# An encoder block: where the forms of the conv rows are made, when raw weights are queued, and how chains of weights are spaced

## The chip, the cores and the metric

The kernel runs on one core of one Trainium2 chip. The metric is device microseconds of one execution; the median of several runs is compared. The engines are TensorE (PE, with its weight loads PEld), VectorE (DVE), ScalarE (ACT), GpSimd (POOL) and SyncE (SP). In this kernel every DMA is issued by SP. Each engine takes its instructions in the order in which the program wrote them, and an instruction that waits for another engine or for a DMA holds up what is behind it on its own engine.

## The reference

One layer on 1024 tokens of width 1024, in float32. What the document needs of it:

```python
u = RMSNorm(x)
q, k, v, cb, cc, ch, ga, gb = split(u @ w_in)
y_a = neighbourhood_attention(q, k, v, rpb) @ w_attn_branch     # 8 heads x 64
y_b = (cb * conv3(cc * ch, conv_w)) @ w_conv_branch             # depthwise, width 3, 512 channels
merged = sigmoid(ga) * y_a + sigmoid(gb) * y_b
x = x + merged @ w_o
x = x + relu(RMSNorm(x) @ w_mlp_in) ** 2 @ w_mlp_out
```

## The kernel before

Every float32 operand is scaled by a power of two and held as two float16 halves, high and low. A product takes three passes of float16 matmuls: high by high, and each high by the other's low. Many products are also done in seven block products in place of eight. For those, both operands are first brought into seven *forms*: four quarters and some of their sums and differences, each split into high and low. The function `seven` runs the seven products of one gate chunk, and its posts add the results up.

The program runs through these stages: norm and the V, Q and K projections (to about 150 us), attention with the conv projections filled in between its steps (to about 315 us), then the stage that the change is about (315 to 572 us: the gates, the two branches and their merging), then W_o, then the MLP. The stage behind attention goes round by round. `gate_units(n)` (line 1444) makes the sigmoid gates of 128 channels out of the chunk S(n), by seven units of twelve matmuls of 128x512. `ab(j)` (line 1538) does the two branches for 256 channels: four A units of twelve matmuls, and seven B units of six matmuls, whose operands are the seven forms of the conv rows. For j from 0 to 2 the order is gate 2j+1, `ab(j)`, gate 2j+2; `ab(3)` follows gate 6, and gate 7 ends the stage.

A unit of work is issued by `unit` (line 235). It writes the matmuls, counts their columns in `work[0]`, writes the posts of the unit before (`settle`), and then calls some `step`s and `tick`s. A step advances every generator in the list `fg`. A tick advances the first generator in the list `bg`; if it answers WAIT, the next one is tried. So a generator's yields decide behind which unit its next instructions stand. `apart(mark, n, of)` answers WAIT until the counter `of` has grown by n; with `of = work` that is a number of columns, and 6144 columns are one unit of twelve matmuls. When the program reaches a point that needs a chunk of weights, `built(chunk)` sets `forced[0]` and ticks until that chunk is split. While forced, `apart` and `aged` don't wait.

The weights come in chunks. Per chunk: `load_upto` (line 263) queues raw loads on SP into five raw buffers of 128x1024 float32. Then `prep_s` (1351, gate chunks S), `prep_b` (1376, chunks B of the conv branch) or `Chunk.prep` with `largest` (361, chunks A of the attention branch) takes the squares or maxima, sums them over the partitions by a matmul with ones (`all_sum`, line 229 in the profile), makes a power of two, makes sums of quarters on POOL (lines 1317 and 1403) and splits into high (ACT, line 1335) and low (DVE, line 1331). `prep_s` and `prep_b` wait until all earlier chunks are done. `aged` (1181) holds a chunk until the columns since its load was queued reach three units.

The conv rows, 512 channels by 1024 tokens, are kept as two halves (a = 0, 1) of four quarters each. Each half becomes seven forms. `hi` (926) copies to float16 on ACT, `lo` (929) subtracts on DVE or POOL, and `put` (932) writes the form to a DRAM buffer `bf`. `land` (1484) reads a form of both halves back from `bf` to one of four slots of `bT`, in the order in which the B units need them: the first four after all forms are put, and each further one after the B unit that used the slot before. Before the change `conv_early` makes three forms of half 0 within attention, staged in `kD`; `conv_late`, advanced one segment a step behind attention, makes the other eleven, with staging tiles in `zb` and `mL` (`M[1]`). Four places in `zb` serve for half 0 first and then for half 1, so that the second use waits for the put of the first. `turn_s(0, 2)` (1301) puts eight DMA transposes on SP's queue between the first and second gate unit.

Of the kernel before, what the change touches and what calls it, by code (L numbers as in the profile page):

```python
# [15 lines left out]
OP = mybir.AluOpType  # L16
# [85 lines left out]
def encoder_block(ctx: ExitStack, tc: tile.TileContext, x, weights, cols, gqk, rel, masks, out):  # L102
# [132 lines left out]
    def unit(mms, post=None, steps=0, ticks=0):  # L235

        for ps, l, r, a, b in mms:
            T.matmul(ps, l, r, start=a, stop=b)  # L238
        units[0] += 1
        work[0] += len(mms) * mms[0][0].shape[-1]  # L240
        settle()
# [17 lines left out]
    def load_into(t, ch, p):  # L259
        m = ch.widths[p][0] * ch.widths[p][1]  # L260
        SP.dma_start(t, bass.AP(tensor=weights.tensor, offset=weights.offset + ch.offs[p], ap=[[m, 128], [1, m]]))
# [631 lines left out]
    SLOT = BTF.rearrange("p (n a w t) -> p n a w t", n=4, a=2, w=2)  # L893
    KS = KD[:, 0:2].rearrange("p a w t -> p (a w t)").rearrange("p (n w t) -> p n w t", n=4, w=2)
    BF = dram.tile([128, 7, 2, 2, 512], F16, name="bf")
    cm, crow, form_tail, formed, rowed = keep(2), at(rowsB, 2, 2), [], [False] * 2, [False]

# [3 lines left out]
    def conv_split(j):  # L901
# [31 lines left out]

    def conv_early():
        (e0, e1), (o0, o1) = quarters(0)
        conv_scaled(0)
        yield
        yield
        for i, v in enumerate((o1, e0, o0)):
            hi(KS[:, i], v)  # L940
            yield
            lo(KS[:, i], v, G)
            yield
        G.tensor_tensor(o1, e1, o1, op=OP.subtract)
        yield
        G.tensor_tensor(e1, e0, e1, op=OP.subtract)
        for i, f in enumerate((3, 0, 1)):
            put(KS[:, i], f, 0)
            yield

    def conv_late():

        zs = zb.rearrange("p n t -> p (n t)").bitcast(F16).rearrange("p (n w t) -> p n w t", n=4, w=2)
        ms = M[1][:, 2:6].rearrange("p n (w t) -> p n w t", w=2)
        (e0, e1), (o0, o1) = quarters(0)
        V.tensor_tensor(e0, o1, e0, op=OP.subtract)
        V.tensor_tensor(o0, o0, e0, op=OP.add)
        conv_scaled(1)
        hi(zs[:, 0], o1), hi(zs[:, 1], e1)
        yield  # L960
        (p0, p1), (q0, q1) = quarters(1)
        V.tensor_tensor(zs[:, 0, 1], o1, zs[:, 0, 0], op=OP.subtract)
        V.tensor_tensor(zs[:, 1, 1], e1, zs[:, 1, 0], op=OP.subtract)
        hi(zs[:, 2], e0), hi(zs[:, 3], o0)
        yield
        lo(zs[:, 2], e0, V), lo(zs[:, 3], o0, V)
        yield
        put(zs[:, 0], 2, 0), put(zs[:, 1], 5, 0)
        hi(ms[:, 0], q1), hi(ms[:, 1], p0), hi(ms[:, 2], q0)
        yield  # L970
        put(zs[:, 2], 4, 0), put(zs[:, 3], 6, 0)
        formed[0] = True
        lo(ms[:, 0], q1, V), lo(ms[:, 1], p0, G), lo(ms[:, 2], q0, G)
        V.tensor_tensor(q1, p1, q1, op=OP.subtract)
        yield
        yield
        V.tensor_tensor(p1, p0, p1, op=OP.subtract)
        V.tensor_tensor(p0, q1, p0, op=OP.subtract)
        hi(ms[:, 3], q1)
        yield  # L980
        put(ms[:, 0], 3, 1), put(ms[:, 1], 0, 1), put(ms[:, 2], 1, 1)
        V.tensor_tensor(q0, q0, p0, op=OP.add)
        hi(zs[:, 0], p1), hi(zs[:, 1], p0)
        yield
        lo(ms[:, 3], q1, V), lo(zs[:, 0], p1, V)
        hi(zs[:, 2], q0)
        yield
        lo(zs[:, 1], p0, V), lo(zs[:, 2], q0, V)
        yield
        put(ms[:, 3], 2, 1), put(zs[:, 0], 5, 1)  # L990
        yield
        put(zs[:, 1], 4, 1), put(zs[:, 2], 6, 1)
        formed[1] = True
# [49 lines left out]
    st = {}  # L1043
# [137 lines left out]
    def aged(ch, i):  # L1181
        return forced[0] or i >= len(ch.when) or work[0] >= ch.when[i] + 3 * 6144

# [44 lines left out]
    def deal(k):  # L1228
        room = 216.0 * share(k) + 520.0
        if conv_tail and not advance(conv_tail[0]):  # L1230
            conv_tail.pop(0)
        if form_tail and not advance(form_tail[0]):
            form_tail.pop(0)
# [51 lines left out]
    V, A = nc.vector, nc.scalar  # L1285
    assert not form_tail and rowed[0]
    solo[0] = False
# [63 lines left out]
    def prep_s(n):  # L1351
# [6 lines left out]
        else:  # L1358
# [10 lines left out]
        yield  # L1369
        ch.P = wsp.tile([128, 7, 2, 512], F16, name="w16_s", tag="ws")  # L1370
# [5 lines left out]
    def prep_b(j):  # L1376
# [10 lines left out]
        yield  # L1387
# [16 lines left out]
        yield  # L1404
        yield
        yield from parts([x for a in range(2) for x in ((place(3, 5, a), w[:, 0, :, a]), (place(5, 7, a), w[:, 1, :, a]))],
# [174 lines left out]
    fg.append(first_forms())  # L1581
    bg.append(prep_s(1))
    bg.append(prep_b(0))
    for j in range(1, 4):
# [6 lines left out]
    sgs[0] = gate_units(0)  # L1591
    gates[0] = 1
    built(cA[0])
# [63 lines left out]
    flush()  # L1657
    side[0] = False

# [616 lines left out]
```

## Time and profile before

| | us |
|---|---|
| median of 3 runs | 1240.71 (1240.1 to 1242.06) |
| the profiled execution, its time | 1241.13 |
| the profiled execution, its span | 1239.4 |
| TensorE busy in it | 1199.1 (97%) |
| DVE, ACT, POOL busy in it | 963.5, 778.1, 486.0 |

The profile is one execution. Its page has the busy time of each engine, a picture of the span in 40 slices, the chain of work that ended last, and the costliest groups of instructions; further views list a stretch of time row by row. A timeline row has its start and its duration in us, the engine, the line in the kernel, the operation, what it writes and reads, its shape, how many instructions it stands for, and in brackets how long the engine was idle before it and what ended that. SPq is the queue of SP: a transfer stands there from the first issue to the last one of its group. PEclk is the clock that TensorE was granted, as a share of full speed. The forms of a matmul with ones (line 229) are small, but TensorE waits for their input like for any other.

### The profile page before, as it was taken

How to read it: one execution, taken by the hardware profiler on the slowest of the kernel's cores; microseconds unless marked ns; L12 is line 12 of the kernel's file. 1: busy time of each engine (PE TensorE's matmuls, PEld its weight loads, DVE VectorE, ACT ScalarE, POOL GpSimd, SP SyncE). 2: the span in 40 equal slices, each digit the busy share in tenths (PEclk: the TensorE clock that was granted, in tenths of full speed). 3: DMA queues.
4: the chain of work that ended last, by engine and by line, in shares of the span. 5: the costliest groups of instructions: out<-in, count | busy, mean ns of one | idle time of the engine just before them, and what ended most of it. 6: DMA issues, size and time to landing. Idle time of an engine off the chain costs nothing.

```text
span 1239.4 us, 17137 instructions
## 1 busy us (share of the span) xinstructions
PE 1199.1 (97%) x6248; PEld 576.3 (46%) x6248; DVE 963.5 (78%) x1790; ACT 778.1 (63%) x1241; POOL 486.0 (39%) x317
## 2 busy tenths in 40 slices
PE   8999999999887789999999999999999999999998
PEld 7444445445433334444448544444444444444444
DVE  7987788888767677688788755554547999999998
ACT  7775678777565546244677877877857663545430
POOL 5610021231333243220002666556557564474472
PEclk9999999999988889999999999999999999999999
DMA  7755646777664142326169454543575843436212
GB/s 261 204 147 111 117 105 122 156 168 129 158 214 159 52 169 68 120 103 235 37 119 205 143 184 158 187 147 134 187 259 191 292 170 131 180 106 251 81 55 103
DMA packets 168373, 189.62 MB, mean 153 GB/s; under 512 B 123616, under 2 KB 124128, under 8 KB 164192
## 3 DMA queue, kind: packets, MB, share of 16 engines
q1 hardware_dynamic: 168288, 188.52, 51.0%
q8 instruction: 49, 0.80, 0.3%
q14 instruction: 36, 0.29, 0.1%
HBM read 117.19 MB, written 41.42 MB: 128 GB/s over the span
## 4 chain that ended last, share of the span: by engine, by line
PE 79%; DVE 10%; ACT 5%; POOL 2%; DMA 1%; issue 1%; SPq 1%; ACTq 0%; POOLq 0%; DVEq 0%
PE ps_d L238 24%; PE ps_s L238 20%; PE ps_o L238 18%; PE ps_d L1156 9%; PE ps_d L675 2%; PE ps_d L724 2%; PE ps_s L724 2%; PE ps_s L675 1%; DVE w_wb L1331 1%; PE ps_o L1137 1%; DVE w_s L1331 1%; PE ps_s L1061 1%; ACT w_s L1335 1%; POOL raw L1403 1%; POOL sg L1534 1%
## 5 line engine op out<-in xcount | busy, mean ns | idle before, releaser
L238 PEld LDWEIGHTS <-ops 128*128 128x128 f16 x1356 | 132.4, 98 | 157.3
L238 PEld LDWEIGHTS <-w 128*128 128x128 f16 x1368 | 132.9, 98 | 139.4
L1156 PE MATMUL ps_d<-uT,w_ws 128*128 128x512 f16 x576 | 128.3, 380 | 0.0
L238 PE MATMUL ps_s<-ops 128*128 128x512 f16 (+1 forms) x528 | 119.7, 377 | 0.0
L238 PE MATMUL ps_d<-ops 128*128 128x512 f16 x480 | 110.1, 379 | 0.0
L2097 ACT ACTIVATE ops<-hf,sc 128x2048 f16<-128x2048 f32 x26 | 52.0, 1999 | 84.8 <-PE ps_s L238 37.7
L1317 POOL TENSOR_TENSOR tsum<-raw 128x512 f32<-128x512 f32 x28 | 48.2, 1737 | 139.1 <-DVE v L1725 74.2
L238 PEld LDWEIGHTS <-w_s 128*128 128x128 f16 x588 | 58.5, 100 | 91.1 <-issue 23.8
L1675 POOL TENSOR_TENSOR as<-as 128x512 f32<-128x512 f32 x60 | 82.9, 1382 | 41.6 <-ACT as L1957 38.1
L1156 PEld LDWEIGHTS <-w_ws 128*128 128x128 f16 x576 | 54.6, 98 | 65.4 <-issue 1.5
L238 PE MATMUL ps_d<-u2T,w 128*128 128x512 f16 (+1 forms) x360 | 78.8, 368 | 0.0
L238 PE MATMUL ps_o<-ops 128*128 128x512 f16 (+1 forms) x348 | 78.6, 375 | 0.0
L1191 ACT ACTIVATE raw<-raw,sc 128x256 f32<-128x256 f32 x164 | 67.9, 494 | 16.8 <-DMA raw<-in_weights 16.8
L2099 DVE SCALAR_TENSOR_TENSOR ops<-hf,sc,ops 128x2048 f16<-128x2048 f32 x26 | 74.6, 2869 | 3.2 <-ACT ops L2097 3.2
L238 PE MATMUL ps_o<-u2T,w 128*128 128x512 f16 (+1 forms) x348 | 76.0, 368 | 0.0
L238 PE MATMUL ps_s<-u2x,w 128*128 128x512 f16 (+1 forms) x336 | 74.5, 371 | 0.0
L1534 POOL TENSOR_TENSOR sg<-sg 128x512 f32<-128x512 f32 x14 | 19.9, 1433 | 116.2 <-DVE sc L232 52.9
L1335 ACT ACTIVATE w<-raw,sc 128x512 f16<-128x512 f32 (+1 forms) x28 | 24.6, 927 | 50.6 <-DVE sc L481 50.6
L1990 DVE TENSOR_TENSOR as<-ps_s,as 128x512 f32<-128x512 f32 x13 | 9.0, 692 | 57.9 <-ACT as L2009 57.9
L2113 POOL TENSOR_TENSOR raw<-raw 128x1024 f32<-128x1024 f32 x8 | 30.8, 3870 | 36.6 <-DVE ops L2107 36.6
L238 PEld LDWEIGHTS <-mH 128*128 128x128 f16 x304 | 29.6, 98 | 30.4
L2071 POOL TENSOR_TENSOR t<-raw,w2x 128x1024 f32<-128x1024 f32 x6 | 19.2, 3204 | 61.5 <-DMA w2x<-in_weights 35.8
(431 smaller groups left out, 2761.5 us busy)
## 6 DMA issues: line engine op xcount, KB each, us to landing
raw<-in_weights SPq DMA_DIRECT2D x89, 512.0 KB, 5.1
hs<-as SPq DMA_DIRECT2D x16, 1792.0 KB, 8.1
hf<-hs SPq DMA_DIRECT2D x26, 1024.0 KB, 6.2
bT<-bf SPq DMA_DIRECT2D x28, 512.0 KB, 5.1
w2x<-in_weights SPq DMA_DIRECT2D x16, 512.0 KB, 7.7
raw<-in_weights SPq DMA_DIRECT2D x16, 384.0 KB, 3.8
xt<-in_x SPq DMA_DIRECT2D x8, 512.0 KB, 11.2
gs<-s SPq DMA_DIRECT2D x4, 1024.0 KB, 4.4
```

The source lines that it names most:

```text
L238: T.matmul(ps, l, r, start=a, stop=b)
L675: T.matmul(ps, UT[:, sa, k, b * 128:(b + 1) * 128], w, start=(kind, k) == ("hh", 0), stop=(kind, k) == ("hl", 7))
L724: T.matmul(vbank["q", b], UT[:, sa, k, b * 128:(b + 1) * 128], cQ.parts[:, sw, 512 * k:512 * k + 512], start=(k, n) == (0, 0), stop=(k, n) ...
L1156: T.matmul(ps, l, r, start=a, stop=b)
L1191: A.activation(v, v, AF.Copy, scale=sc[:, at(g, 4 * i + k)])
L1317: G.tensor_tensor(t[:, o], a, b, op=OP.add)
L1335: A.activation(o(0), w, AF.Copy, scale=sc[:, scale(n)])
L1534: G.tensor_tensor(t, t, part(n, 2 * half + 1), op=OP.add)
L1675: sub.tensor_tensor(z[o], z[a], z[b], op=op)
L2097: A.activation(P[:, 1, 0], hf, AF.Copy, scale=sc[:, Rs])
L2099: V.scalar_tensor_tensor(P[:, 1, 1], hf, sc[:, Rs], P[:, 1, 0], op0=OP.mult, op1=OP.subtract)
L2113: G.tensor_tensor(w11[i2], w11[i2], w12[i2], op=OP.add)
```

## The change

1. *Forms.* `conv_early` is gone, with its generator in the attention loop and its staging in `kD`. `conv_late` makes all fourteen forms, and each has a staging tile of its own: four in `zb`, six in `mH` and four in `mL`. The scaling of each half by `conv_scaled` is called right at the end of its `conv_split`. Of the fourteen remainders four are made on POOL and ten on DVE, and all eight differences and sums on DVE; before, it was five and nine (three of the five in attention), and two differences on POOL and six on DVE. The first put comes at step 7 of `conv_late` in place of 4, the last at step 13 in place of 12.
2. *Loads.* From behind the first gate units to the end of the stage, `load_upto` notes the request with the column count at which it is due, 9216 columns (one and a half units) later. `due` carries due requests out, in `unit` before the posts, and at once while forced.
3. *Chains.* `aged` waits for two units since the load was queued, not three. In `prep_s` a unit of columns lies between the sums of quarters and the split, where one yield lay, and the wait behind the sum over the partitions is two units in place of three. In `prep_b` two units lie behind the squares (one yield before), the wait behind the sum is three units in place of two for j > 0, and two units (one for j = 0) lie between the sums of quarters and their split, in place of two yields. `prep_b(0)` stands before `prep_s(1)` in `bg`.

```diff
@@ flush and built @@
+            due()
             tick()
             step()
@@ unit @@
         work[0] += len(mms) * mms[0][0].shape[-1]
+        due()
         settle()
@@ loads @@
+    pend, deferring = [], [False]
+
+    def due():
+        while pend and (forced[0] or pend[0][0] <= work[0]):
+            load_now(pend.pop(0)[1])
+
     def load_upto(n):
+        if deferring[0]:
+            pend.append((work[0] + 9216, n))
+        else:
+            load_now(n)
+
+    def load_now(n):
         while loaded[0] < min(n - held[0], limit[0], len(loads)):
@@ conv_split @@
-        if a == 0:
-            form_tail.append(conv_early())
-        else:
-            rowed[0] = True
+        conv_scaled(a)
+        rowed[0] = a == 1
@@ conv_late @@
-        ms = M[1][:, 2:6].rearrange("p n (w t) -> p n w t", w=2)
...
+        ms = [M[i][:, 2 + n].rearrange("p (w t) -> p w t", w=2) for i in range(2) for n in range(6 - 2 * i)]
+        st = [[zs[:, n] for n in range(4)] + ms[:3], ms[3:10]]
         (e0, e1), (o0, o1) = quarters(0)
+        (p0, p1), (q0, q1) = quarters(1)
+        a, b = st
...
+        hi(a[0], o1), hi(a[1], e0), hi(a[2], o0)
+        yield
+        lo(a[0], o1, V), lo(a[1], e0, G), lo(a[2], o0, G)
+        yield
+        sub(o1, e1, o1), sub(e1, e0, e1)
+        hi(b[0], q1), hi(b[1], p0), hi(b[2], q0)
+        yield
+        hi(a[3], o1), hi(a[4], e1)
+        lo(b[0], q1, V), lo(b[1], p0, G), lo(b[2], q0, G)
+        yield
+        sub(e0, o1, e0)
         V.tensor_tensor(o0, o0, e0, op=OP.add)
...
+        yield
+        lo(a[3], o1, V), lo(a[4], e1, V)
+        hi(a[5], e0), hi(a[6], o0)
+        sub(q1, p1, q1), sub(p1, p0, p1)
+        yield
+        puts(a, 0, (0, 3), (1, 0), (2, 1))
+        lo(a[5], e0, V), lo(a[6], o0, V)
+        hi(b[3], q1), hi(b[4], p1)
+        yield
+        sub(p0, q1, p0)
+        V.tensor_tensor(q0, q0, p0, op=OP.add)
+        puts(a, 0, (3, 2), (4, 5))
+        yield
+        lo(b[3], q1, V), lo(b[4], p1, V)
+        hi(b[5], p0), hi(b[6], q0)
+        puts(a, 0, (5, 4), (6, 6))
         formed[0] = True
+        yield
+        puts(b, 1, (0, 3), (1, 0), (2, 1))
+        lo(b[5], p0, V), lo(b[6], q0, V)
+        yield
+        yield
+        puts(b, 1, (3, 2), (4, 5))
+        yield
+        puts(b, 1, (5, 4), (6, 6))
         formed[1] = True
@@ aged @@
-        return forced[0] or i >= len(ch.when) or work[0] >= ch.when[i] + 3 * 6144
+        return forced[0] or i >= len(ch.when) or work[0] >= ch.when[i] + 2 * 6144
@@ prep_s @@
-            s, ch.inv = yield from scale_of(am, 9, 3)
+            s, ch.inv = yield from scale_of(am, 9, 2)
...
         yield from forms_sum(ch, t, None)
-        yield
+        yield from apart(work[0], 6144, work)
@@ prep_b @@
-        yield
+        yield from apart(work[0], 2 * 6144, work)
         am = sum_of(sm)
         yield
-        s, ch.inv = yield from scale_of(am, 0, 2)
+        s, ch.inv = yield from scale_of(am, 0, 3 if j else 2)
...
-        yield
-        yield
+        yield from apart(work[0], 2 * 6144 if j else 6144, work)
@@ the stage @@
-    bg.append(prep_s(1))
-    bg.append(prep_b(0))
+    bg.extend([prep_b(0), prep_s(1)])
...
-    gates[0] = 1
+    gates[0], deferring[0] = 1, True
...
-    side[0] = False
+    side[0] = deferring[0] = False
```

More of the change, by code (lines that the diff above doesn't have):

```diff
@@ L240, in unit @@
         work[0] += len(mms) * mms[0][0].shape[-1]
+        due()
         settle()
@@ L893, in encoder_block @@
     SLOT = BTF.rearrange("p (n a w t) -> p n a w t", n=4, a=2, w=2)
-    KS = KD[:, 0:2].rearrange("p a w t -> p (a w t)").rearrange("p (n w t) -> p n w t", n=4, w=2)
     BF = dram.tile([128, 7, 2, 2, 512], F16, name="bf")
-    cm, crow, form_tail, formed, rowed = keep(2), at(rowsB, 2, 2), [], [False] * 2, [False]
+    cm, crow, formed, rowed = keep(2), at(rowsB, 2, 2), [False] * 2, [False]
     def quarters(a):
@@ L932, in put, with conv_late, sub, puts @@
         SP.dma_start(BF[:, f, a], t)
-    def conv_early():
+    def conv_late():
+        zs = zb.rearrange("p n t -> p (n t)").bitcast(F16).rearrange("p (n w t) -> p n w t", n=4, w=2)
+        ms = [M[i][:, 2 + n].rearrange("p (w t) -> p w t", w=2) for i in range(2) for n in range(6 - 2 * i)]
+        st = [[zs[:, n] for n in range(4)] + ms[:3], ms[3:10]]
         (e0, e1), (o0, o1) = quarters(0)
-        conv_scaled(0)
+        (p0, p1), (q0, q1) = quarters(1)
+        a, b = st
+        def sub(o, x, y):
+            V.tensor_tensor(o, x, y, op=OP.subtract)
+        def puts(t, a, *nf):
+            for n, f in nf:
+                put(t[n], f, a)
+        hi(a[0], o1), hi(a[1], e0), hi(a[2], o0)
[9 more added lines that the diff above has]
+        sub(e0, o1, e0)
+        V.tensor_tensor(o0, o0, e0, op=OP.add)
+        yield
[14 more added lines that the diff above has]
+        puts(a, 0, (5, 4), (6, 6))
+        formed[0] = True
+        yield
+        puts(b, 1, (0, 3), (1, 0), (2, 1))
+        lo(b[5], p0, V), lo(b[6], q0, V)
@@ L937, in conv_early @@
         yield
         yield
-        for i, v in enumerate((o1, e0, o0)):
-            hi(KS[:, i], v)
-            yield
-            lo(KS[:, i], v, G)
-            yield
-        G.tensor_tensor(o1, e1, o1, op=OP.subtract)
-        yield
-        G.tensor_tensor(e1, e0, e1, op=OP.subtract)
-        for i, f in enumerate((3, 0, 1)):
-            put(KS[:, i], f, 0)
-            yield
-    def conv_late():
-        zs = zb.rearrange("p n t -> p (n t)").bitcast(F16).rearrange("p (n w t) -> p n w t", n=4, w=2)
-        ms = M[1][:, 2:6].rearrange("p n (w t) -> p n w t", w=2)
[L955 to L959, printed above, removed]
-        yield
[L961 to L992, printed above, removed]
@@ L1231, in deal @@
             conv_tail.pop(0)
-        if form_tail and not advance(form_tail[0]):
-            form_tail.pop(0)
         for n in range(4):
@@ L1285, in encoder_block @@
     V, A = nc.vector, nc.scalar
-    assert not form_tail and rowed[0]
+    assert rowed[0]
     solo[0] = False
@@ L1368, in prep_s @@
         yield from forms_sum(ch, t, None)
-        yield
+        yield from apart(work[0], 6144, work)
         ch.P = wsp.tile([128, 7, 2, 512], F16, name="w16_s", tag="ws")
```

3 lines of the change are left out of this document (removed).

## The prediction

> **What bounds the kernel now.** I read the windows view first, in four stretches: late attention, the attention stretch with lost TensorE time, the first two thirds of the stage behind attention, and its last third. The columns are each engine's busy time, then the granted TensorE clock and the DMA share.
>
> ```profile
> span 1239.4 us, 17137 instructions
> ...
> 230.00:255.00 25.00, 25.00 (x185) 12.45 (x185) 24.45 (x68) 20.27 (x50) 8.26 (x7) 1.00 0.71 149
> 255.00:275.00 20.00, 17.39 (x127) 8.80 (x126) 17.60 (x50) 14.35 (x36) 7.32 (x10) 0.92 0.83 177
> 314.00:480.00 166.00, 136.49 (x590) 58.92 (x589) 120.64 (x251) 95.16 (x170) 60.53 (x48) 0.91 0.44 139
> 480.00:566.00 86.00, 85.68 (x399) 38.70 (x398) 63.42 (x119) 36.10 (x54) 17.33 (x14) 1.00 0.31 100
> ```
>
> TensorE is the bound nearly everywhere, so only its pauses can be won. From 314 to 480 it is idle for 29.5 of 166 us at a mean clock of 0.91. From 480 on the same kind of units run without a pause. The change edits exactly this stage, so I listed its pauses in the timeline of TensorE (start, duration, group; in brackets the idle time before it and what ended it).
>
> ```profile
> 333.56 0.16 PE L229 MATMUL ps_d<-ones 128*128 128x1 bf16 x1 [3.21 <-DVE ones L1169]
> 333.59 4.26 PE L238 MATMUL ps_s<-uT,w_s 128*128 128x512 f16 x12
> ...
> 346.97 0.18 PE L229 MATMUL ps_d<-ones 128*128 128x1 bf16 x1 [1.35 <-DMA bf<-mL]
> ...
> 358.24 0.19 PE L229 MATMUL ps_s<-ones 128*128 128x1 bf16 x1 [3.24 <-DVE sc L232]
> 358.29 2.72 PE L238 MATMUL ps_d<-bT,w_wb 128*128 128x512 f16 x6
> 360.80 2.77 PE L238 MATMUL ps_s<-bT,w_wb 128*128 128x512 f16 x6
> ...
> 381.72 2.74 PE L238 MATMUL ps_d<-bT,w_wb 128*128 128x512 f16 x6 [7.53 <-DMA bT<-bf]
> ...
> 425.09 0.16 PE L229 MATMUL ps_s<-ones 128*128 128x1 bf16 x1 [6.83 <-DVE ones L376]
> 425.12 4.57 PE L238 MATMUL ps_o<-s4T,w_s 128*128 128x512 f16 x12
> 429.53 1.46 PE L238 MATMUL ps_d<-bT,w_wb 128*128 128x512 f16 x6
> ...
> 432.14 2.75 PE L238 MATMUL ps_d<-qD,w_wa 128*128 128x512 f16 x12
> ...
> 453.97 5.28 PE L238 MATMUL ps_d<-uT,w_s 128*128 128x512 f16 x12 [4.12 <-DVE zb L1549]
> ...
> 477.96 2.32 PE L238 MATMUL ps_o<-uT,w_s 128*128 128x512 f16 x10 [2.27 <-DVE sg L1478]
> ```
>
> Twelve matmuls undisturbed take 2.75 us and six take 1.46, as listed. After a long pause the first groups take longer, which is the lowered clock, and I add that excess to the pause. This gives seven losses:
> A, at 333: 3.21 + (4.26 - 2.75) = 4.7. B, at 347: 1.35. C, at 358: 3.24 + (2.72 - 1.46) + (2.77 - 1.46) = 5.8. D, at 381: 7.53 + (2.74 - 1.46) = 8.8. E, at 425: 6.83 + (4.57 - 2.75) = 8.65. F, at 454: 4.12 + (5.28 - 2.75) = 6.65. G, at 478: 2.27. Together 38.3 us: this is all that there is to win here.
>
> Next the queue of SP, which issues every transfer, in its order.
>
> ```profile
> 321.16 5.96 SPq L261 DMA_DIRECT2D raw<-in_weights  x3
> 327.21 10.36 SPq L1304 DMA_TRANSPOSE uT<-gs  x8
> 337.62 2.06 SPq L932 DMA_DIRECT2D bf<-zb  x4
> ...
> 346.90 1.86 SPq L1487 DMA_DIRECT2D bT<-bf  x4
> ...
> 361.04 2.88 SPq L1487 DMA_DIRECT2D bT<-bf  x2
> 369.39 7.86 SPq L261 DMA_DIRECT2D raw<-in_weights  x3
> 377.34 7.47 SPq L1487 DMA_DIRECT2D bT<-bf  x5
> ...
> bT<-bf SPq DMA_DIRECT2D x28, 512.0 KB, 5.1
> ```
>
> Loss D can be read here. The landing of the seventh form stands behind three raw loads, the last of which waits for its buffer until about 377.3. A landing takes 5.1 us, and TensorE goes on at 381.7.
>
> **The change part by part. 1, the forms.** The rows that price it: first groups of instructions of one tile or line (count, then min/median/max in ns, first and last start), then three rows of the timeline.
>
> ```profile
> L926 ACT ACTIVATE mL<-bT x4: 616/617/617, 328.2 to 333.5; 128x512 f16<-128x512 f32 x4
> L929 POOL TENSOR_TENSOR kD<-bT,kD x3: 1156/1157/1452, 238.1 to 253.9; 128x512 f16<-128x512 f32 x3
> L944 POOL TENSOR_TENSOR bT<-bT x1: 1590/1590/1590, 259.2 to 259.2; 128x512 f32<-128x512 f32 x1
> L946 POOL TENSOR_TENSOR bT<-bT x1: 1460/1460/1460, 260.9 to 260.9; 128x512 f32<-128x512 f32 x1
> L929 DVE TENSOR_TENSOR zb<-bT,zb x5: 684/692/693, 323.6 to 345.8; 128x512 f16<-128x512 f32 x5
> ...
> 329.61 1.54 DVE L974 TENSOR_TENSOR bT<-bT 128x512 f32<-128x512 f32 x1
> ...
> 333.42 0.68 DVE L977 TENSOR_TENSOR bT<-bT 128x512 f32<-128x512 f32 x1
> ...
> 340.06 1.33 ACT L926 ACTIVATE zb<-bT 128x512 f16<-128x512 f32 x2 [4.37 <-DMA bf<-zb]
> ```
>
> Attention loses five POOL operations (3 x 1.16 to 1.45, 1.59, 1.46: 6.8 us), three ACT copies and three puts. TensorE runs full there except for the one stretch with 20 - 17.39 = 2.6 us idle and a clock of 0.92, another 0.08 x 20 = 1.6. Bounds of the gain: 0 to 4.2; I take 1, because the last of these operations ends at 262.4, early in that stretch.
>
> Behind attention the same work is added: three ACT copies (1.85), one DVE remainder and two DVE differences (3 x 0.69 = 2.1), two more POOL remainders (2 x 1.16 to 1.45). ACT and DVE are 57% and 73% busy there, so this is hidden by their waits. Uncovered it would be 2.1 on DVE. A DVE difference took 1.54 us beside a POOL operation and 0.68 without, so each added POOL remainder may also stretch a DVE operation by 0.86: I add 1 us (0 to 1.7).
>
> The Trainium skill, page "SBUF — State Buffer", section "Who interferes with whom", says that a DVE instruction with two SBUF inputs and a POOL instruction that reads SBUF exclude each other for a whole instruction. By that rule the two POOL remainders would cost DVE up to their full length, and the estimate in place of 1 would be up to 2.9; the trace agrees in kind, with its 1.54 against 0.68.
>
> What goes away is the wait of ACT at 340. One staging tile was reused, its put stood in SP's queue behind eight transposes (327.2 to 337.6), and ACT stood for 4.37 us with the chains of weights queued behind it. Those feed B and C. With prep_b(0) now ahead of prep_s(1), the squares that end A's wait are also issued earlier, while prep_s(1)'s two loads, which stood ahead of the transposes, fall behind them; the transposes can start near 321.5. I take A, B and C as gone: -11.9 (bounds 0 and -11.9).
>
> What is late next is the first four landings. They were issued at 346.9, when the first B unit still had 11.4 us to go. That unit would come about 10 us earlier, and three more puts (some 0.5 each from 4 in 2.06) and one step more stand ahead of the landings; but the queue moves up by up to 5.7. Cost +3 (0 to 6).
>
> **2, the deferred loads.** In ab(0) the raw loads that delay D are requested in one A unit (twelve matmuls of 512 columns). With 9216 columns of delay they are issued after the next A unit, hence behind the seventh form's landing, which then goes out when the third B unit is read (about 368) and is there at 373: D gone, -8.8 (0 to -8.8). Within the gate units SP holds hardly anything but raw loads, so delay there changes only their place in the list, not the wait for their buffer. Where a chain is forced, loads are queued at once. New on SP: a raw load now waits behind landings, which wait for TensorE.
>
> **3, the spacing.** E and F are in-order queues blocked by chains issued in one burst. For F, four rows of the timeline, and one of the chain of waits with the length of a unit of twelve:
>
> ```profile
> 441.33 2.95 POOL L1317 TENSOR_TENSOR gsum<-raw 128x512 f32<-128x512 f32 x2
> ...
> 448.73 1.15 ACT L1335 ACTIVATE w_s<-gsum,sc 128x1024 f16<-128x1024 f32 x1 [3.27 <-POOL gsum L1317]
> ...
> 449.92 1.28 DVE L1331 SCALAR_TENSOR_TENSOR w_s<-gsum,sc,w_s 128x1024 f16<-128x1024 f32 x1 [2.34 <-ACT w_s L1335]
> ...
> 453.24 0.68 DVE L1549 TENSOR_TENSOR zb<-ps_d,zb 128x512 f32<-128x512 f32 x1
> ...
> 480.71 2.59 PE ps_d L238 x12
> ```
>
> POOL makes the sums, ACT waits 3.27 for them, DVE 2.34 for ACT, and L1549, which frees a bank for TensorE, is queued behind. A whole unit, 2.59 us in the chain of waits, now lies between sums and split. It covers 2.34 of this, but POOL began the sums late for other reasons; of F I take half, -3.3 (0 to -6.65). E is a DVE queue that runs several units behind after the burst of prep_b(1); prep_b now spreads over columns. Half again, -4.3 (0 to -8.65). G stays.
>
> The price: a B chain gets longer by 0.5 (load and age), 2, 1 and about 1.6 units, 5.1 x 2.59 = 13 us. It then needs about 14.5 units: 1.5 + 2 + 2 + 3 + 1, one for the scale, 1 + 2 + 1 for the parts. A round has 14 gate units, 4 A units and 7 half units, 21.5. So it fits, with some seven units to spare, unless an earlier chunk holds it up. I allow one forced chain at the price of C: +5.8 (0 to 17.4 for three).
>
> **The sum**, against the profiled execution's 1241.1 us: -1 + 1 - 11.9 + 3 - 8.8 - 3.3 - 4.3 + 5.8 = -19.5, hence **1222 us**. The median of the runs is 0.4 lower, which is within the rounding. A cross-check: the stretch of 166 us would last about 147 with DVE at (120.6 + 2.1) / 147 = 83%. TensorE ran full at 74% DVE (63.42 of 86) and at 98% (24.45 of 25), so DVE does not forbid it.
>
> **The rivals.** First, the landings take over: A to C turn into one wait of the first B units. For it speaks that 11.4 us of cover are about what A, B and C would take away, against it that the transposes move up. Then -11.9 and +3 fall away: 1241.1 - 10.6 = 1231.
>
> Second, nothing: the weights are not split when they are asked for, so the forced loops skip every spacing and delay. Only A to C are won, 11.9 - 3, and one and a half forced chains (8.7) eat them: 1241. For it speaks that A, B and C are forced matmuls today; against it that from 480 on the same chains keep up.
>
> Third, slower: raw loads arrive too late. A load goes out behind landings, the chain behind it starts half a unit later and a B chain is 13 us longer, and later chunks wait for earlier ones. If B chains are forced in all three later rounds at E's price, +26, against -11.9 + 3 - 8.8 - 3.3 = -21 with the halves of E not won: 1246. It decides against the change from the point where a chain takes over 21.5 units. For it speaks that only five raw buffers serve six loads a round.
>
> The Trainium skill, page "DMA: Bandwidth & Descriptors", section "Rules for kernel authors", tells to issue a transfer early and wait for it late. By that rule alone this third case is the right one; the D rows speak against it, since there an early load held up a transfer that was needed sooner.
>
> **How the numbers follow.** Forecast 0.52 (its own range 1210 to 1231), landings 0.18, nothing 0.10, slower 0.20. A measurement here tells about 0.2%, or 2.5 us, from no change: faster 0.70, same 0.10, slower 0.20. The range is 1208 to 1243: it takes in the first three cases and the near side of the fourth.
>
> **What would show it.** Right: no ACT wait for a put of forms; the transposes of uT in SP's queue start near 321; no TensorE wait of over 2 us for bT; the pauses between 314 and 480 fall from 29.5 to about 13 us, with the clock nearer 1. Wrong: new matmuls with ones that wait for DVE between 480 and 566, ACT waiting for raw loads, or the first B unit waiting for bT. The prediction falls if TensorE's idle time in this stage stays above 25 us, or if time outside it moves by more than 4.

## The result, and the profile after

The changed kernel took 1223.38 us (median of four runs, 1222.02 to 1223.72) against 1241.02 for the kernel before (1240.1 to 1242.06). The ratio is 0.9856, with a 95% interval of 0.9839 to 0.9873. The forecast of 1222.0 with its range of 1208 to 1243 held. The profiled execution of the changed kernel took 1222.02 us and had a span of 1220.2.

The windows view of the changed kernel, for the same four stretches as in the prediction. Columns: us, busy time of PE, PEld, DVE, ACT and POOL with the number of instructions, granted clock, DMA share, GB/s.

```profile
230.00:255.00 25.00, 25.00 (x184) 12.43 (x183) 23.68 (x72) 19.68 (x49) 7.20 (x7) 1.00 0.81 159
255.00:275.00 20.00, 20.00 (x147) 9.96 (x145) 17.19 (x57) 15.92 (x40) 2.02 (x5) 1.00 0.75 157
314.00:480.00 166.00, 145.94 (x656) 64.19 (x655) 130.99 (x268) 102.76 (x182) 56.94 (x46) 0.96 0.45 147
480.00:566.00 86.00, 86.00 (x402) 38.98 (x401) 67.90 (x125) 35.92 (x55) 17.71 (x15) 1.00 0.45 162
```

From 314 to 480 us TensorE is now idle for 166 - 145.94 = 20.1 us (29.5 before), at a clock of 0.96 (0.91). The stretch of attention that had 2.6 us idle is full, and so is the last third of the stage. DVE is busy 131 of 166 us, more than the 120.6 of before, because more of the stage falls into the same 166 us.

The timeline of TensorE in the changed kernel, with the start of the first gate unit and all pauses of more than a microsecond in the stage behind attention:

```profile
309.93 5.34 PE L240 MATMUL ps_o<-uT,w_ws 128*128 128x512 f16 x24
...
327.60 0.61 PE L240 MATMUL ps_s<-uT,w_s 128*128 128x512 f16 x2 [1.96 <-ACT w_s L1338]
329.79 4.45 PE L240 MATMUL ps_s<-uT,w_s 128*128 128x512 f16 x10 [1.58 <-DVE w_s L1334]
...
335.99 2.33 PE L240 MATMUL ps_d<-qD,w_s 128*128 128x512 f16 x10 [0.90 <-DVE w_s L1334]
...
367.69 1.47 PE L240 MATMUL ps_d<-bT,w_wb 128*128 128x512 f16 x6 [2.97 <-DMA bT<-bf]
...
385.35 0.16 PE L231 MATMUL ps_s<-ones 128*128 128x1 bf16 x1 [3.22 <-DVE ones L1174]
387.07 0.16 PE L231 MATMUL ps_d<-ones 128*128 128x1 bf16 x1 [1.56 <-DVE ones L1174]
387.10 4.13 PE L240 MATMUL ps_s<-qD,w_s 128*128 128x512 f16 x12
...
449.36 2.75 PE L240 MATMUL ps_s<-s4T,w_s 128*128 128x512 f16 x12 [2.35 <-DVE sc L234]
...
465.11 0.16 PE L231 MATMUL ps_d<-ones 128*128 128x1 bf16 x1 [5.23 <-DVE ones L391]
465.13 4.36 PE L240 MATMUL ps_s<-uT,w_s 128*128 128x512 f16 x12
...
477.13 1.46 PE L240 MATMUL ps_s<-bT,w_wb 128*128 128x512 f16 x6
```

Counted as the prediction counted its seven losses, with the excess of slow groups: the start of gate 1 costs 1.96 + 1.58 + 0.90 + (4.45 - 2.33) = 6.6 (A was 4.7); B and C are gone; the wait for bT costs 3.0 (D was 8.8); E is gone, but gate 2 has a new pause of 3.22 + 1.56 + (4.13 - 2.75) = 6.2; F is gone, with 2.35 left in gate 4; G is gone, but gate 5 has a new pause of 5.23 + (4.36 - 2.75) = 6.8. Together 24.9 us in place of 38.3, so 13.4 won. The first gate unit starts at 309.93, and before at 314.65: 4.7 won ahead of the stage.

SP's queue in the changed kernel, from the transposes on:

```profile
316.47 0.34 SPq L264 DMA_DIRECT2D raw<-in_weights  x1
316.86 10.35 SPq L1307 DMA_TRANSPOSE uT<-gs  x8
...
344.02 3.03 SPq L1489 DMA_DIRECT2D bT<-bf  x4
351.34 0.33 SPq L264 DMA_DIRECT2D raw<-in_weights  x1
352.65 1.61 SPq L1489 DMA_DIRECT2D bT<-bf  x2
359.44 1.92 SPq L264 DMA_DIRECT2D raw<-in_weights  x2
361.45 0.38 SPq L1489 DMA_DIRECT2D bT<-bf  x1
```

The transposes start 6.9 us behind the first gate unit (12.6 before). But the landing of the seventh form still goes out behind two raw loads (359.44, 361.45).

### The profile page after: what moved, and what is told of

Same layout as the page of the kernel before. It is cut to its first block, busy times and chain, and to the rows that moved or that the text cites. A ratio compares the mean times of both kernels' runs of the same rounds, so it can differ in the third digit from the quotient of the medians.

```text
span 1220.2 us, 17138 instructions
## 1 busy us (share of the span) xinstructions
PE 1191.6 (98%) x6248; PEld 573.6 (47%) x6248; DVE 959.1 (79%) x1793; ACT 777.6 (64%) x1241; POOL 479.9 (39%) x314
## 4 chain that ended last, share of the span: by engine, by line
PE 79%; DVE 12%; ACT 4%; POOL 2%; issue 2%; DMA 2%; DVEq 0%; ACTq 0%; POOLq 0%
PE ps_d L240 23%; PE ps_s L240 19%; PE ps_o L240 17%; PE ps_d L1161 10%; DVE w_s L1334 2%; PE ps_d L690 2%; PE ps_d L739 2%; PE ps_s L739 2%; DVE w_wb L1334 2%; PE ps_s L690 1%; PE ps_o L1142 1%; PE ps_s L1066 1%; DMA raw<-in_weights 1%; POOL sg L1536 1%; DVE sc L381 1%
## 5 line engine op out<-in xcount | busy, mean ns | idle before, releaser
L2104 ACT ACTIVATE ops<-raw,sc 128x1024 f16<-128x1024 f32 x24 | 26.3, 1138 | 26.6 <-DVE sc L152 19.2
```

## The experiments

Ratios are to the kernel before on the same chip, with 95% intervals.

### The three parts alone, and each left out

Six kernels take parts 1 (forms), 2 (loads) and 3 (chains) of the change singly and in pairs.

**Forms alone.** Against the kernel before:

```diff
-        if a == 0:
-            form_tail.append(conv_early())
-        else:
-            rowed[0] = True
+        conv_scaled(a)
+        rowed[0] = a == 1
...
+        puts(a, 0, (0, 3), (1, 0), (2, 1))
```

> The kernel before with part 1 alone (all forms behind attention, a staging tile each). Theory, each part takes away its own losses: the 4.7 us that attention got shorter belong to this part, and so do some of the pauses at 347 and 358 of the old trace; expected 1241 - 4.7 - about 4 = 1232, with the wait of ACT for a put gone. Rival, the parts only work together: the transposes of uT still stand behind the two raw loads of the forced S chain, more puts follow them, and the first B unit waits for its form: the 4.7 us of attention alone or less, 1236 to 1241.

Measured: 1236.93 us, 0.9966 (0.9955 to 0.9978). TensorE's timeline:

```profile
331.33 0.16 PE L229 MATMUL ps_d<-ones 128*128 128x1 bf16 x1 [5.50 <-DVE ones L1159]
...
377.05 2.74 PE L238 MATMUL ps_d<-bT,w_wb 128*128 128x512 f16 x6 [12.35 <-DMA bT<-bf]
```

B and C are gone, but the wait for bT grows from 7.53 to 12.35 and A from 3.21 to 5.50. For this part alone the first rival was right: the landings take over. What is left of the gain is about what attention gives.

**Loads alone.** Against the kernel before:

```diff
     def load_upto(n):
+        if deferring[0]:
+            pend.append((work[0] + 9216, n))
+        else:
+            load_now(n)
```

> The kernel before with part 2 alone (raw loads queued 9216 columns later, ageing still three units). Theory: the pause of 7.5 us for bT in the first round is gone, 1241 - 6 to - 9 = 1232 to 1235, and the rest of the trace stays. Rival: the S and A chains start one and a half units later, with an ageing of three units on top, so that forced chains cost as much as the landing wins or more: 1239 to 1250.

Measured: 1241.32 us, 0.9998 (0.9988 to 1.0009), as the rival had it. No wait for bT of any size is left, so loss D goes. But the chains, which still wait three units behind the load, now start four and a half units behind the request, and the gain is given back at matmuls with ones, this one above all:

```profile
472.55 0.16 PE L231 MATMUL ps_s<-ones 128*128 128x1 bf16 x1 [10.66 <-DVE sc L1183]
```

**Chains alone.** Against the kernel before:

```diff
-        return forced[0] or i >= len(ch.when) or work[0] >= ch.when[i] + 3 * 6144
+        return forced[0] or i >= len(ch.when) or work[0] >= ch.when[i] + 2 * 6144
...
-        yield
+        yield from apart(work[0], 6144, work)
...
-    bg.append(prep_s(1))
-    bg.append(prep_b(0))
+    bg.extend([prep_b(0), prep_s(1)])
```

> The kernel before with part 3 alone (order of the first two chains, spacing by columns, ageing of two units). Theory: the pauses at 425 and 454 of the old trace shrink by half and the one at 333 goes, 1241 - 4.7 - 7.6 = about 1229, while the pause for bT stays. Rival: with forms and loads as before, the longer B chains are forced more often: 1238 to 1250.

Measured: 1232.25 us, 0.9932 (0.9917 to 0.9947). This is the largest part by itself, and E is gone. Of what was expected, A did not go (2.01 and 1.61 us, with ten slow matmuls behind), and the wait for bT did not stay (0.49). It has one large new pause, of a matmul with ones that TensorE meets before its input is there:

```profile
377.75 0.16 PE L229 MATMUL ps_d<-ones 128*128 128x1 bf16 x1 [11.74 <-DVE ones L1169]
```

**All but the loads.** Against the changed kernel:

```diff
     def load_upto(n):
-        if deferring[0]:
-            pend.append((work[0] + 9216, n))
-        else:
-            load_now(n)
-
-    def load_now(n):
         while loaded[0] < min(n - held[0], limit[0], len(loads)):
```

> The changed kernel without part 2 (raw loads queued at once). Theory: the pause for bT in the first round comes back to about 8 us where the changed kernel has 3.0, so 1223 + 5 to + 6 = 1229. Rival: with chains spaced by columns the raw loads are requested at other places and no longer stand ahead of the landing that is needed: 1221 to 1224, and the deferral is not what removed it.

Measured: 1229.27 us, 0.9907 (0.9892 to 0.9921), so the deferral is worth 5.9 us on top of the other two. The time is the one that the theory expected, but not for the reason of step D:

```profile
376.04 0.16 PE L229 MATMUL ps_d<-ones 128*128 128x1 bf16 x1 [12.84 <-DVE ones L1159]
...
380.53 1.46 PE L238 MATMUL ps_s<-bT,w_wb 128*128 128x512 f16 x6 [0.35 <-DMA bT<-bf]
```

The long pause is again a matmul with ones, of a chain of weights for later. The landing is late as well (its queue moves at 376), but behind this pause it costs only 0.35.

**All but the forms.** The kernel before with the diffs of the loads and of the chains above.

> The changed kernel without part 1 (forms made as before, three of them in attention, staging shared). Theory: part 1 alone took 4.1 us off, nearly all in attention, and its staging should take more off where the chains are spaced, so the changed kernel loses 5 to 8: 1223 + 5 to 8 = 1228 to 1231, with the pause in attention near 270 back and ACT waiting for a put again. Rival: only attention's 4.7 come back, 1227 to 1228, and the shared staging costs nothing where chains are spaced.

Measured: 1225.29 us, 0.987 (0.9855 to 0.9885), less than either expectation. On top of the other two parts the forms are worth 1.9 us, less than the 4.7 that attention gives.

**All but the chains.** The kernel before with the diffs of the forms and of the loads.

> The changed kernel without part 3 (forms behind attention and loads deferred, chains as before, ageing three units). Theory: deferring needs the spaced chains, as part 2 alone gave nothing: forms alone were 1237, and here 1235 to 1239, with pauses of TensorE before matmuls with ones. Rival: the deferral takes the 12 us pause for bT of the run with forms alone away, 1226 to 1230.

Measured: 1234.98 us, 0.9948 (0.9931 to 0.9964), with pauses at matmuls with ones of 5.50, 6.00 and 9.34 us and none for bT.

Put together, the parts don't add up: forms -4.1, loads 0, chains -8.8 alone make -12.9, and all three make -17.6. Most of the loads' gain needs the chains: it is 5.9 us with both other parts, 7.0 with the chains alone (1232.25 to 1225.29), some 2 with the forms alone (1236.93 to 1234.98) and none by itself.

### Attention

The kernel before with the five POOL operations of its early forms left out: three remainders and two differences are not computed, so the forms made from them hold wrong values.

```diff
             hi(KS[:, i], v)
             yield
-            lo(KS[:, i], v, G)
             yield
-        G.tensor_tensor(o1, e1, o1, op=OP.subtract)
         yield
-        G.tensor_tensor(e1, e0, e1, op=OP.subtract)
```

> The kernel before with the five POOL operations of the early forms in attention left out (three remainders and two differences, so three forms hold other data, and two forms made of them are wrong); their ACT copies and puts stay. Theory, POOL beside DVE is what cost attention 4.7 us: the pause near 270 goes, attention ends 4 to 5 us earlier, 1236 to 1237. Rival, the ACT copies or the puts did it: attention as before, 1240 to 1241.

Measured: 1239.52 us, 0.9978 (0.9963 to 0.9993). The first gate unit:

```profile
312.17 5.13 PE L238 MATMUL ps_o<-uT,w_ws 128*128 128x512 f16 x23
```

It starts at 312.17: 2.5 of the 4.7 us come from these five operations, which take 6.8 us of POOL. The time lies between the two expectations. With the ACT copies and puts gone too (forms alone), it is 310.13.

From 236 to 272 us DVE has the same operations in the same order in the kernel before and in this run, but not in the same time. Here are two of them, first in the kernel before, where POOL's two differences (1.59 us at 259.2 and 1.46 at 260.9) run beside them, then in this run:

```profile
260.18 2.56 DVE L97 SCALAR_TENSOR_TENSOR w_ws<-raw,sc,w_ws 128x384 f16<-128x384 f32 x2
...
259.25 1.13 DVE L97 SCALAR_TENSOR_TENSOR w_ws<-raw,sc,w_ws 128x384 f16<-128x384 f32 x2
```

In the kernel before DVE doesn't catch up: the operation that it starts at 270.05, just before TensorE's pause ends at 270.71, starts at 267.69 here, 2.4 us earlier. So POOL's time beside DVE costs these 2.5 us. The other 2.0 go with the ACT copies, the puts and the order of the work around them, which were not told apart.

### Later chains in place of later loads

The change without its deferral, but with 21504 columns (3.5 units) between load and chain in place of 2 units. A load is queued at once, and a chain starts where the deferral by 1.5 units would let it start.

```diff
-            pend.append((work[0] + 9216, n))
...
-        return forced[0] or i >= len(ch.when) or work[0] >= ch.when[i] + 2 * 6144
+        return forced[0] or i >= len(ch.when) or work[0] >= ch.when[i] + 21504
```

> The changed kernel with raw loads queued at once, but every chain still starting 3.5 units after its load was requested, as in the changed kernel. The chains are issued at the same places; only the place of the raw loads in SP's queue differs. Theory, it is the queue order: landings stand behind raw loads again, a pause of 6 to 9 us for bT in the first round, 1228 to 1230. Rival, it is the start of the chains: without deferral the matmul with ones of the first round went out 12 us early; here it does not, 1222 to 1225.

Measured: **1215.7 us**, 0.9792 (0.9778 to 0.9807), 7.7 us faster than the changed kernel and less than either expectation. SP's queue has raw loads and landings in the same order as in the changed kernel all through this stage. So what pays against the changed kernel isn't the place of the loads in the queue, but the later start of the chains. What differs from the changed kernel are the chains whose loads were queued before the deferral begins or while a chain is forced: they start 2 units behind the request there, and 3.5 here.

### The mirror: loads later, chains early

The changed kernel with its deferral, and half a unit between load and chain:

```diff
-        return forced[0] or i >= len(ch.when) or work[0] >= ch.when[i] + 2 * 6144
+        return forced[0] or i >= len(ch.when) or work[0] >= ch.when[i] + 3072
```

> The changed kernel with one constant smaller: raw loads are still queued 9216 columns (1.5 units of twelve matmuls) after their request, but a chain starts 3072 columns after its load was queued in place of 12288, so 2 units after the request as in the run without the deferral (1229.3 us) and not 3.5 as in the changed kernel (1223.4). Theory, the start of the chains decides: about 1229 us (1226 to 1232), with the long wait of a matmul with ones in gate 2 back (over 8 us). Rival, the place of the raw loads in SP's queue decides: about 1223 us (1221 to 1225), as the loads stand where they stand in the changed kernel.

Measured: 1237.71 us, 0.9969 (0.9959 to 0.9979). Both numbers were missed; the direction is that of the start of the chains.

```profile
375.34 0.16 PE L231 MATMUL ps_s<-ones 128*128 128x1 bf16 x1 [10.72 <-DVE ones L1174]
402.82 0.16 PE L231 MATMUL ps_s<-ones 128*128 128x1 bf16 x1 [6.86 <-DVE ones L1174]
...
453.45 5.23 PE L240 MATMUL ps_s<-uT,w_s 128*128 128x512 f16 x12 [5.20 <-DVE zb L1549]
```

The long pauses at matmuls with ones are back, and F too. The expectation had overlooked the loads that are not deferred: their chains start half a unit behind the request here.

### Later still

4.5 units between load and chain, no deferral:

```diff
-        return forced[0] or i >= len(ch.when) or work[0] >= ch.when[i] + 21504
+        return forced[0] or i >= len(ch.when) or work[0] >= ch.when[i] + 27648
```

> The run with 3.5 units between load and chain and no deferral (1215.7 us), with 4.5 units (27648 columns) in its place. Theory, the start of the chains decides: the early matmuls with ones go on losing, but B chains come a unit closer to being forced; 1213 to 1222 us, and the 6.0 us wait of the matmul with ones in gate 2 gets shorter. Rival, any delay between request and chain is as good as another above 3.5 units, and what is left is DVE's and ACT's own work: 1215 to 1217 us.

Measured: 1219.96 us, 0.9826 (0.981 to 0.9842). It is 4.3 us slower than 3.5 units, but still faster than the changed kernel. The pause in gate 2 did not get shorter (6.32 against 6.01); a wait for bT of 2.25 at 424 and one of 2.38 for DVE at 477 are new.

### The first prepared gate chunk without its unit

The run with 3.5 units, where `prep_s(1)` splits right behind its sums:

```diff
-        yield from apart(work[0], 6144, work)
+        yield from apart(work[0], 6144 if n > 1 else 0, work)
```

> The same run with 3.5 units and no deferral (1215.7 us), but in the first prepared gate chunk alone, prep_s(1), the unit of 6144 columns between its sums and its split is taken out; all other chains keep it. Theory, that unit makes the pauses at the start of gate 1 (1.50, 0.38 and 2.87 us there): they go and 1211 to 1213 us come out. Rival, these weights are late because DVE and ACT are full with the forms (L926 and L941 stand ahead of them): the split starts earlier but the forms are late in its place, 1215 to 1217 us, and the first wait for bT, 2.02 us there, grows.

Measured: 1222.67 us, 0.985 (0.9831 to 0.9869), 7.0 us slower. The pauses at gate 1 do go, as the theory said, but the time doesn't follow. The queue of SP shows the price:

```profile
317.12 7.81 SPq L261 DMA_DIRECT2D raw<-in_weights  x3
325.03 10.36 SPq L1292 DMA_TRANSPOSE uT<-gs  x8
...
346.23 3.32 SPq L1474 DMA_DIRECT2D bT<-bf  x4
...
366.17 7.67 SPq L1474 DMA_DIRECT2D bT<-bf  x5
```

The earlier split asks for its raw loads earlier, so that three of them stand ahead of the eight transposes, which start at 325.03 in place of 317.28. The first landings go out at 346.23 in place of 341.36. TensorE then waits 3.49 us for the put of a form, and 1.19, 1.75 and 4.18 for bT. The rival had the kind of loss right (the forms are late in its place) and its size wrong.

### The same start for all chains, with the deferral

The changed kernel, where a load that wasn't deferred counts as queued 9216 columns later. All chains then start 3.5 units behind the request. TensorE, DVE, ACT and POOL have the same instructions in the same order as in the run of 1215.7 us; in this stage only SP's queue differs.

```diff
-            load_now(pend.pop(0)[1])
+            load_now(pend.pop(0)[1], forced[0])
...
-    def load_now(n):
+    def load_now(n, early=True):
...
-            ch.when.append(work[0])
+            ch.when.append(work[0] + 9216 * early)
```

> The changed kernel with its deferral of raw loads, but a load that was queued without deferral (before the stage, or while a chain is forced) counts as queued 9216 columns later. Every chain then starts 3.5 units after its request, as in the run with no deferral and 3.5 units (1215.7 us): TensorE, ACT, DVE and POOL have the same instructions in the same order as there, and only SP's queue differs, where raw loads now stand behind landings of the forms. Theory, the start of the chains decides and the place in SP's queue is worth little: 1214 to 1218 us. Rival one, step D of the prediction, raw loads ahead of a landing cost TensorE: the wait of 2.02 us for bT at 366 goes, and 1212 to 1214 us come out. Rival two, raw loads that go out later come too late for the chains: 1219 to 1224 us, as in the changed kernel (1223.4), with ACT waiting for raw.

Measured: **1213.88 us** (1213.79 to 1214.94), 0.9783 (0.9766 to 0.98), in the range of rival one and at the edge of the theory's. This is the fastest of all, 9.5 us below the changed kernel, from which it differs only in the start of the early chains. It is 1.8 us below the run that queues loads at once, or 1.1 by the ratios, and their intervals overlap: the place of the raw loads in the queue is worth some 1 to 2 us, which the times alone don't show clear of noise. The later start of the early chains is worth the 9.5 us. SP's queue and TensorE's timeline:

```profile
352.59 5.52 SPq L1489 DMA_DIRECT2D bT<-bf  x3
358.46 2.54 SPq L264 DMA_DIRECT2D raw<-in_weights  x2
...
413.54 5.53 SPq L1489 DMA_DIRECT2D bT<-bf  x3
```

```profile
334.28 4.02 PE L240 MATMUL ps_d<-qD,w_s 128*128 128x512 f16 x10 [2.87 <-DVE w_s L1334]
...
381.42 0.16 PE L231 MATMUL ps_s<-ones 128*128 128x1 bf16 x1 [8.11 <-DVE ones L1174]
...
431.50 2.75 PE L240 MATMUL ps_d<-uT,w_s 128*128 128x512 f16 x12
...
468.64 1.46 PE L240 MATMUL ps_s<-bT,w_wb 128*128 128x512 f16 x6
```

The third landing of its group now goes ahead of the two raw loads, and no wait for bT is left. For comparison, the run that queues loads at once, TensorE first and then SP's queue:

```profile
366.12 1.47 PE L238 MATMUL ps_d<-bT,w_wb 128*128 128x512 f16 x6 [2.02 <-DMA bT<-bf]
...
381.37 0.16 PE L229 MATMUL ps_s<-ones 128*128 128x1 bf16 x1 [6.01 <-DVE ones L1159]
...
429.62 2.74 PE L238 MATMUL ps_s<-bT,w_wb 128*128 128x512 f16 x6 [2.06 <-DVE sg L1511]
```

```profile
424.74 0.33 SPq L261 DMA_DIRECT2D raw<-in_weights  x1
425.12 7.59 SPq L1474 DMA_DIRECT2D bT<-bf  x5
```

In the first round the wait for bT goes and nothing is won: the matmul with ones in gate 2 starts at 381.37 there and at 381.42 here, because DVE has its input ready at the same time, and the pause there grows from 6.01 to 8.11. What the queue does win comes a round later. There a landing stands behind a raw load until 425.12, and TensorE waits until 429.62; here it goes out ahead of that raw load, by 419.1, and the same matmuls start at 427.61. (The row names DVE, but the same operation of DVE starts at 428.89 here, after TensorE has gone on, and there the weight loads of that unit wait 2.6 us for bT.)

Against the changed kernel: gate 4 starts at 431.50 here and at 431.29 in the changed kernel; the round behind gate 5 starts at 468.64 and at 477.13. So the whole gain over the changed kernel comes in gates 4 and 5, where the pauses of 2.35 and 6.8 are gone. The pause in gate 2 is still there, and with 8.11 us it is the largest that is left.

All runs with forms and spaced chains, by the start of the chains:

| chains start behind the request, in units: loads not deferred / other loads | loads queued at once | loads deferred |
|---|---|---|
| 0.5 / 2 | | 1237.7 |
| 2 / 2 | 1229.3 | |
| 2 / 3.5 | | 1223.4 (the change) |
| 3.5 / 3.5 | 1215.7 | 1213.9 |
| 4.5 / 4.5 | 1220.0 | |

## Why the prediction was right or wrong

The time was right (1222.0 against 1223.4), but by steps whose errors cancel, so the hit is in good part luck. The prediction gave 1 us to attention and 18.5 to the stage behind it. By the profiles attention gave 4.7, and the stage 14.8: W_o begins at 552.35 in place of 571.89, which is 19.5 earlier. Step by step:

1. **Attention, -1: measured -4.7**, outside its bounds of 0 to 4.2. It was right that the loss lies near the stretch from 255 to 275: 4.5 of the 4.7 us are won between 266 and 280. The step that failed is the one that took 1 us of it because the last POOL operation ends at 262.4. DVE, which POOL had slowed, is still 2.4 us late when TensorE waits for it at 270.71. Five POOL operations of 6.8 us alone cost attention 2.5 us.
2. **POOL beside DVE, +1:** no run measured this by itself.
3. **A to C, -11.9: measured -5.3.** B and C went, ACT's wait for a put went, and the transposes moved up. A did not go: the step "the squares that end A's wait are also issued earlier" was right about the squares, but behind them the split of the same weights is late (6.6). One piece of this is the unit that the change puts between sums and split, which the prediction weighed only for F. The run that takes it out there shows that the pauses go with it, and that they cover something else.
4. **Landings, +3: measured 0 for the first four.** They go out at 344.02, and the first B unit, at 351.17, waits for nothing.
5. **D, -8.8: measured -5.8**, from 8.8 to 3.0. Here the mechanism failed, not only the size. The prediction said that the raw loads would be queued behind the seventh landing; in the changed kernel two still go out ahead of it. Nor is such a wait a loss that can be taken off by itself: with the loads alone it was gone and the time stayed the same, and in the last run, against that of 1215.7 us, the 2.02 us that went came back as 2.10 more in gate 2. That a raw load ahead of a landing can cost TensorE is right, but it shows a round later, at 429.62, and with everything else equal the loads' place is worth 1 to 2 us. The deferral works mainly because it lets chains start later, which in part 2 the prediction didn't count at all; under part 3 it counted the longer chain as a price. The Trainium skill, page "DMA: Bandwidth & Descriptors", section "Rules for kernel authors", tells to issue a transfer early and wait late. By that rule the run that queues at once and starts its chains late is the better one. It is, against the changed kernel (1215.7 against 1223.4); with the same start of the chains the later issue was no slower (1213.9).
6. **E and F by half, -7.6: measured -6.8.** Of F 2.35 is left, in gate 4; E is gone, but gate 2 has 6.2 in its place. **G, 0: measured +4.6**, as gate 5 has 6.8 in place of 2.27. The three together gave 2.2. The step that failed is "G stays": a queue that is blocked in one place less was blocked in another.
7. **One forced B chain, +5.8: not found.** The new pauses are at matmuls with ones whose inputs aren't there yet, in front of which DVE has other work. Chains that are late, which were feared, would be looked for with 4.5 units; that run is 4.3 us slower than the one with 3.5 and still faster than the changed kernel. What costs is chains that start too early.

Steps 3 to 6 sum to some -13.3 by the pauses listed, and the stage gave 14.8. Most of the rest lies in pauses and slow matmuls too small for the list: over the whole stage TensorE's idle time fell from 29.8 to 20.1 us, and half of its busy time at the lowered clock from 10.5 to 5.7, together by 14.5.

Of the rivals, "landings take over" is what the forms do alone. "Slower" came out in none of the runs with the chains spaced. Of the conditions at the end of the prediction, the idle time fell below 25 (to 20.1, not to 13), and no new pause came behind 480; ACT does wait for raw loads, but for 5.4 us where it waited 16.8 before, and in the runs of 1213.9 and 1215.7 us not at all. But "no wait of over 2 us for bT" failed (2.97), and so did "time outside the stage moves by no more than 4" (4.7). By its own condition, then, the account fell although the time was hit.

What isn't settled: why gate 2 keeps a pause at matmuls with ones in the changed kernel (4.8 us) and in the runs with 3.5 and 4.5 units (6.01 to 8.11). In the changed kernel DVE's sums of squares stand there behind the merging of the round before, as its timeline shows:

```profile
379.21 0.15 DVE L1438 TENSOR_SCALAR sc<-sc 128x1 f32<-128x1 f32 x1 [2.73 <-ACT mL L1436]
...
383.75 1.28 DVE L1443 SCALAR_TENSOR_TENSOR mL<-sg,sc,mH 128x1024 f16<-128x1024 f32 x1 [1.23 <-ACT mH L1441]
...
385.14 0.16 DVE L1174 CAST ones<-sc 128x1 bf16<-128x1 f32 x1
```

That taking this merging from in front of the sums would end the pause was not tried.

## What to carry to other kernels

On an engine that takes its instructions in order, work for later that is issued too early stops the work for now: a matmul with ones of 0.16 us held TensorE for up to 12.84 us. So tune the distance between a load and the first use of its data apart from the place where the load is queued, try it on both sides, and make sure that it holds for every load, those before the stage too. And when an earlier step frees a buffer, look at which transfers it moves ahead of others in a shared queue: winning 4.75 us of pauses cost 7.0 us net here. And a wait that a change removes isn't yet time won: the 2.02 us for bT came back one gate on, where TensorE waits for DVE.

## What the runs showed of the hardware

What a pause does to TensorE's clock depends on where it falls, and not on its length alone. In all fourteen profiles the granted clock falls to 0.50 for 3.41 us, or for two or three times that, and in each profile all these pieces lie on one grid with steps of 3.41 us. I cut the traces along this grid, from 225 to some 583 us, which gives 1378 pieces at full clock. Behind every piece in which TensorE was idle for 2.06 us or more the clock is halved, and behind none with 1.92 us or less; of the five between, four were followed by the lowered clock. Two examples show it, with TensorE's busy time and clock in each piece: first the run of 1215.7 us, then the changed kernel.

```profile
426.23:429.65 3.42, 1.36 (x8) 1.00 0.93 371
429.65:433.06 3.41, 3.41 (x9) 0.50 0.92 377
...
362.61:366.02 3.41, 2.11 (x10) 1.00 0.79 246
366.02:369.43 3.41, 1.74 (x9) 1.00 0.31 105
369.43:372.84 3.41, 3.41 (x18) 1.00 1.03 412
```

The first pause, of 2.06 us, lies within one piece, and the six matmuls behind it took 2.74 us in place of 1.46. The second, of 2.97 us, is cut by the boundary at 366.02 into 1.3 and 1.7 us, and the six matmuls behind it took 1.47. The Trainium skill, page "TensorE: Matmul & The Clock Gate", section "Why this matters for your kernels", tells to leave no idle gaps of over about 3 us between bursts of matmuls; here a gap of 2.06 us was enough to lower the clock, and one of 2.97 us did not.
